# Head norm of an RWKV-7 step: mean taken off the values ahead of the scans, scale, offset and bonus in feature rows

## The chip, the cores and the metric

One core of a Trainium2 chip runs the whole step as one program. The metric is the device time of one execution in microseconds; lower is better. Three runs of the kernel before are given, and one execution was recorded by the hardware profiler.

## What is computed

One layer of a diffusion backbone on 128 context tokens and 1024 latent tokens, 1024 model columns, in float32. After a norm, one projection feeds two groups of heads: eight RWKV-7 heads of 64 (two directions), and a bidirectional RG-LRU. Their outputs are concatenated, projected, added to the input, and a gated ConvFFN follows. The change concerns the RWKV-7 heads after their scan:

```python
def _wkv7_step(S, inp):                     # S: values (i) x keys (j)
    r_t, w_t, kk_t, b_t, k_t, v_t = inp
    sa = jnp.einsum('dbhij,dbhj->dbhi', S, kk_t)
    S = S * w_t[..., None, :] - sa[..., :, None] * b_t[..., None, :] + v_t[..., :, None] * k_t[..., None, :]
    y = jnp.einsum('dbhij,dbhj->dbhi', S, r_t)
    return S, y
...
    s_fin, y = lax.scan(_wkv7_step, s0.astype(f32), xs)
    o = merge_dirs(y)
    mu = jnp.mean(o, axis=-1, keepdims=True)
    var = jnp.mean(jnp.square(o - mu), axis=-1, keepdims=True)
    o = ((o - mu) * lax.rsqrt(var + LNX_EPS)).reshape(bsz, T, WA) * lnx_g + lnx_b
    bonus = jnp.sum(rh[None] * kdh * r_k, axis=(0, -1))[..., None] * vh
    out = (o + bonus.reshape(bsz, T, WA)) * g
```

The step is linear in the values and in the first state, along the value index `i`. The latents start from a cached state; the context starts from zero, and its final states are an output.

## The kernel before

Tokens stand in nine tiles of 128 (tile 0 the context), heads in four pairs `f` of 128 features. Intermediate results go through DRAM tensors (`r_d`, `k_d`, `kk_d`, `v_d`, `kb_d`, `tt_d`, `g_d`, `y_d` and others). Most DMAs are issued by SP's queue in order, some by ACT's. Python generators mark pauses, and `beside_all` or the `Background` streams take turns among them; this sets the order in which the work is written out. The tile framework then places instructions on the engines' queues and adds all waits, so that an engine runs its own queue in order.

**Projection with background work** (`p_xwxa`, `p_k`, `p_r`, `p_v`, `p_g`). A block of the projection is 128 columns for all tokens, in three spans of 384 tokens (`SPAN`), each of 24 products. The order of the blocks' weights is in `ORDER`; `wtile` loads two blocks ahead and splits one ahead. Before, the blocks are xwxa, k0, r0, k1, r1, v0, k2, r2, v1, k3, r3, v2, v3 and the gelu blocks g0 to g2 (`EARLY`). `p_v` (L774) copies a span of values to `vt` and, with each chunk of 64 tokens reversed, to `vr`, transposes both in 128-token pieces to token rows (L788) and stores them in `v_d`. After `p_k(f)` the stream `unit_keys(f)` is pushed, after `p_r(f)` the stream `stage_ab(f)` (L521). `stage_ab` works on three groups of tokens (128, 512, 512) and two directions: rates, keys, decay powers, scaled keys, and products for the triangular inverses. `bonus` (L613) sums the keys of both directions times the queries over each head: a product with a two-column operand `rkc`, then `cols2` (L437), which copies the two rows by ACT and transposes them back to columns in `bon_f[f]`. At its end `stage_ab` pushes `inverse`, whose elimination runs on DVE. Each yield of the projection advances `stage_ab` by 4 steps, the inverses by 3, the unit keys by 2. Tiles named `ag` share 10 buffers; a group and its two directions take 9.

**Second half of the projection** (`rest_of_projection`, L965) runs beside lanes a and b of the scans: RG-LRU blocks, their gates and scans, g3, and the gate of the RWKV heads.

**Four lanes.** Each lane is a `chain` (L1074) over chunk pairs; both directions and both heads of a pair run together. First states of the latents are transposed by a product with `ident` (L1117). Beside the lanes run the rest of the modulation (`mod_rest`), the RG-LRU half of the output projection (`wout_lru`), and the posts. A post (L1251) handles two latent tiles of a head pair that both directions have completed (16 posts), or two head pairs of the context (2 posts). With tokens on the partitions it takes the mean off (L1278 to L1280), squares on ACT, sums (L1284), computes `rstd`, multiplies value by bonus (L1282) and adds the offset (L1286), multiplies by `rstd` (L1288) and scale (L1289), adds both (L1291), transposes on PE (L1295) and multiplies by the gate (L1296). It has five steps; `posts(90)` takes them in turn with the lanes, `bg_p.finish()` the rest. `PO` and `V` are both DVE.

**Output projection, second norm, FFN** follow, tile by tile in the order `seq_t`.

Of the kernel before, what the change touches and what calls it, by code (L numbers as in the profile page):

```python
# [19 lines left out]
T = 1152  # L20
# [10 lines left out]
def beside_all(*gens):  # L31
    """Advance the streams so that each has done the same share of its work."""
    st = [[g, float(n), 0] for g, n in gens]
    while st:
        s = min(st, key=lambda e: e[2] / e[1])
        try:
            next(s[0])
            s[2] += 1
            yield
        except StopIteration:  # L40
            st.remove(s)
# [17 lines left out]
def tile_hybrid_step(  # L59
# [12 lines left out]
    spill_a = nc.scalar.dma_start  # of what the activation engine has written  # L72
# [7 lines left out]
    def deal(**m):  # L80
        """Which of the eight banks each stream takes in turn."""
# [12 lines left out]
    def mm3(out, l, r, start=True, stop=True):  # L94
        """float32 product of operands given as two 12-bit parts (hi, lo)."""
# [7 lines left out]
    def round_hi(eng, hi, src):  # L103
        """src rounded to 12 bits."""
# [5 lines left out]
    def rest_lo(eng, lo, src, hi):  # L110
        """What the rounding left, which again fits into 12 bits."""
        eng.tensor_tensor(lo, src, hi.bitcast(F32), op=OP.subtract)  # L112

    def vhalf(n, d):
        """Half of the partitions that holds the values of chunk n of a pair; the other half holds the corrections."""
        return n if d == 0 else 1 - n
# [7 lines left out]
    def rstd(pool, ss, n, inv, eps, name):  # L124
        """(ss * inv + eps) ** -0.5 on [128, n], one Newton step on top of sqrt and reciprocal."""
# [21 lines left out]
    # values by chunk pair of either direction  # L147
# [5 lines left out]
    # what the first half of a chain leaves to the second: partial outputs and states  # L153
    o_d = dp.tile([4, 4, 128, 256], F32, name="o_d")
    s_d = dp.tile([4, 128, 256], F32, name="s_d")
    # per head pair and chunk pair: scaled keys and queries, and the inverses
# [14 lines left out]
    # ================================================================== first norm and input projection  # L171
# [17 lines left out]
    # of the inverses, which end later  # L189
# [31 lines left out]
    ROWS2 = [("lru_conv_w", 16), ("lru_conv_b", 4), ("ffn_conv_b", 44)]  # L221
# [38 lines left out]
    # keep: zero at the first token of each chunk, for running sums that start anew there  # L260
# [4 lines left out]
    # ------------------------------------------------------------------ conditioning columns  # L265
# [31 lines left out]
    def scaled(name, src, n, mul, add=0.0):  # L297
# [10 lines left out]
    rkc = const("rkc", 128, 4, 2)  # L308
    rkh = scaled("rkh", col("rw_r_k", 0, 4), 4, 0.5)
    V.tensor_tensor(rkc, rkh.unsqueeze(2).to_broadcast([128, 4, 2]),  # L310
                    hsel.unsqueeze(1).to_broadcast([128, 4, 2]), op=OP.mult)
    # softplus(-lam) = max(-lam, 0) + log1p(exp(-|lam|)), log1p(e) = 2 atanh(e / (2 + e))
# [21 lines left out]
    def mod_cols(idx, row, nr, n):  # L334
        """n * 128 columns of the modulation (two rows, or four with the low parts) to the partitions."""
# [16 lines left out]
    # ------------------------------------------------------------------ first norm  # L352
# [57 lines left out]
    def low_rank(f):  # L410
        """Both low-rank products' weights of a head pair: hi on both halves, lo on one."""
# [19 lines left out]
    # ------------------------------------------------------------------ RWKV: what the chains need of one head pair  # L431
    pc_f = [pc_pool.tile([128, 2, 18], F32, name=f"pc{f}") for f in range(4)]
    bon_f = [pc_pool.tile([128, 18], F32, name=f"bon{f}") for f in range(4)]
# [3 lines left out]
    def cols2(dst, src, lhs, b):  # L437
        """lhs' src, two rows, to pairs of columns."""
# [12 lines left out]
    def inverse(ds, off_, nu, done):  # L451
        """Inverses of the unit triangles of nu units per partition group, in two steps: the 32 x 32 diagonal blocks by
        elimination with one unit per partition, then the off-diagonal block."""
# [67 lines left out]
    def stage_ab(f):  # L521
        # decay, the scaled keys and queries of the chunks, and the products for the inverses
        low = low_rank(f)
        ds, off_ = ab4("ds"), iv("off", "off", 2)

        class Group:
            """Tokens of one direction: the context, or half of the latents."""
# [1305 lines left out]
```

## Time and profile before

| | us |
|---|---|
| runs of the kernel before | 1878.15, 1882.23, 1889.5 (median 1882.23) |
| span of the profiled execution | 1891.5 |
| PE busy in it | 1737.6 |
| DVE busy in it | 1327.0 |
| ACT, POOL busy in it | 850.8, 842.2 |

The span runs from the first to the last instruction of the profiled execution; the page gives no other time for that execution. PE is TensorE's products, PEld its weight loads, DVE VectorE, ACT ScalarE, POOL GpSimd, SP the queue that issues most DMAs. A product of float32 operands stands as two PE records, a transpose or a product of float32r operands as one. `mm<-h_hi,winh` names the written tile and the read ones.

### The profile page before, as it was taken

The page shows a single profiled execution, that of the slowest core. Times are in us where ns is not written, and L with a number is a line of the kernel's source. Part 1 is how long each engine was busy: PE and PEld are TensorE (multiplying, and loading weights), DVE is VectorE, ACT ScalarE, POOL GpSimd, SP SyncE. Part 2 cuts the span into 40 slices and gives each one's busy share as a digit, 9 for nine tenths or more (in the row PEclk, how much of TensorE's full clock was granted, in tenths as well). Part 3 has the DMA queues.
Part 4 walks back from the last instruction along what each step waited for, and adds up shares of the span by engine and source line. Part 5 has one row for each costly group of instructions (what it writes and reads, how often), then busy time and mean ns, then how long its engine had stood idle before and what let it go on. Part 6 is the DMA issues. An engine that isn't in the chain of part 4 may idle for free.

```text
span 1891.5 us, 36156 instructions
## 1 busy us (share of the span) xinstructions
PE 1737.6 (92%) x13421; PEld 1465.4 (77%) x13421; DVE 1327.0 (70%) x2669; ACT 850.8 (45%) x1759; POOL 842.2 (45%) x866
## 2 busy tenths in 40 slices
PE   6998899989999999789997869999999999999996
PEld 5876677778677778456664769999999999788885
DVE  5457887796567664578997967666677778567764
ACT  6345444432557467555542854444444443121211
POOL 1144554532354354353332066666666665344340
PEclk9999898888989899899996989999999999999998
DMA  8344544432533333877765412222222224648571
GB/s 251 104 151 141 161 131 155 153 125 96 164 94 116 115 101 100 261 213 241 239 190 182 152 34 85 80 77 76 71 76 71 70 82 153 191 150 272 169 253 60
DMA packets 276702, 264.94 MB, mean 140 GB/s; under 512 B 21253, under 2 KB 226720, under 8 KB 276528
## 3 DMA queue, kind: packets, MB, share of 16 engines
q1 hardware_dynamic: 260864, 245.99, 41.8%
q10 hardware_dynamic: 15376, 16.52, 2.6%
q8 instruction: 106, 1.74, 0.4%
q14 instruction: 68, 0.56, 0.1%
q0 software_dynamic: 288, 0.14, 0.0%
HBM read 188.00 MB, written 74.58 MB: 139 GB/s over the span
## 4 chain that ended last, share of the span: by engine, by line
PE 42%; DVE 4%; DMA 1%; ACT 1%; POOL 1%; issue 1%; SPq 0%; ACTq 0%; DVEq 0%; POOLq 0%
PE acc L92 13%; PE y L92 7%; PE z L92 7%; PE x L92 7%; PE v L92 3%; PE mm L92 3%; POOL wl L112 1%; PE wo L92 1%; DVE zf L1592 0%; DVE zf L1593 0%; DMA raw<-in_w_up 0%; DVE tm L1381 0%; PE tr L1455 0%; DMA act_d<-zf 0%; ACT xt L1459 0%
## 5 line engine op out<-in xcount | busy, mean ns | idle before, releaser
L92 PE MATMUL mm<-h_hi,winh 128*128 128x384 f32 x528 | 194.1, 368 | 3.4 <-DVE vr L782 2.6
L92 PE MATMUL mm<-h_lo,winh 128*128 128x384 f32 x528 | 191.2, 362 | 0.6 <-DVE h_lo L112 0.6
L92 PE MATMUL mm<-h_hi,winl 128*128 128x384 f32 x528 | 189.1, 358 | 0.0
L112 POOL TENSOR_TENSOR wl<-raw,wh 128x512 fp32r<-128x512 f32 x110 | 154.4, 1405 | 63.4 <-ACT wh L106 57.9
L106 ACT ACTIVATE wh<-raw 128x512 fp32r<-128x512 f32 x110 | 69.3, 632 | 150.3 <-PE z L92 81.0
L92 PEld LDWEIGHTS mm<-h_hi,winh 128*128 128x128 f32 x528 | 105.6, 200 | 15.8 <-issue 8.6
L92 PE MATMUL x<-f_hi,wh 128*128 128x256 f32 (+1 forms) x352 | 105.8, 301 | 9.3 <-ACT q L1625 5.6
L92 PEld LDWEIGHTS mm<-h_lo,winh 128*128 128x128 f32 x528 | 106.2, 201 | 8.5 <-issue 6.2
L112 POOL TENSOR_TENSOR wl<-S,wh 128x512 fp32r<-128x512 f32 x44 | 59.9, 1361 | 113.9 <-ACT wh L106 113.9
L92 PEld LDWEIGHTS mm<-h_hi,winl 128*128 128x128 f32 x528 | 105.8, 200 | 3.5 <-issue 2.4
L92 PE MATMUL x<-f_lo,wh 128*128 128x256 f32 (+1 forms) x352 | 105.5, 300 | 0.2 <-DVE f_lo L112 0.2
L92 PE MATMUL x<-f_hi,wl 128*128 128x256 f32 (+1 forms) x352 | 105.2, 299 | 0.0
L92 PE MATMUL y<-t_hi,wh 128*128 128x320 f32 (+1 forms) x352 | 104.5, 297 | 0.0
L92 PE MATMUL y<-t_lo,wh 128*128 128x320 f32 (+1 forms) x352 | 104.5, 297 | 0.0
L92 PE MATMUL y<-t_hi,wl 128*128 128x320 f32 (+1 forms) x352 | 104.2, 296 | 0.0
L1064 POOL TENSOR_TENSOR BK<-BK,pc 128x256 f32<-128x256 f32 x72 | 50.7, 706 | 110.8 <-PE pa L92 35.0
L108 POOL TENSOR_SCALAR winh<-win 128x512 fp32r<-128x512 f32 x44 | 29.8, 693 | 150.2 <-PE mm L92 92.4
L92 PE MATMUL acc<-f_hi 128*128 128x512 f32 x330 | 88.8, 390 | 3.3 <-ACT zf L1733 3.3
L108 POOL TENSOR_SCALAR t_hi<-raw 128x512 fp32r<-128x512 f32 x66 | 55.3, 840 | 77.1 <-PE acc L92 34.3
L1592 DVE SCALAR_TENSOR_TENSOR zf<-C,fcw,zf 128x567 f32<-128x567 f32 x66 | 63.1, 956 | 23.1 <-ACT zf L1590 23.1
L92 PEld LDWEIGHTS x<-f_hi,wh 128*128 128x128 f32 x352 | 67.8, 193 | 10.3 <-ACT q L1625 6.2
L92 PEld LDWEIGHTS acc<-f_hi 128*128 128x128 f32 x330 | 61.8, 188 | 16.4 <-ACT zf L1733 3.7
(522 smaller groups left out, 5529.0 us busy)
## 6 DMA issues: line engine op xcount, KB each, us to landing
raw<-in_w_down SPq DMA_DIRECT2D x132, 256.0 KB
raw<-in_w_up SPq DMA_DIRECT2D x88, 256.0 KB
wm<-in_w_mod SPq DMA_DIRECT2D x64, 256.0 KB
act_d<-zf SPq DMA_DIRECT2D x44, 288.0 KB
src<-act_d SPq DMA_DIRECT2D x66, 192.0 KB
win<-in_w_in SPq DMA_DIRECT2D x44, 256.0 KB
KR<-kb_d SPq DMA_DIRECT2D x36, 256.0 KB
VS<-v_d SPq DMA_DIRECT2D x36, 256.0 KB
```

The source lines that it names most:

```text
L92: PE.matmul(out, lhsT, rhs, start=start, stop=stop, skip_group_check=True)
L106: A.activation(hi, src, AF.Copy)
L108: eng.tensor_scalar(hi, src, 1.0, 0.0, op0=OP.mult, op1=OP.add)
L112: eng.tensor_tensor(lo, src, hi.bitcast(F32), op=OP.subtract)
L1064: G.tensor_tensor(bk, bk, pc_f[q.f][:, :, x:x + 1].to_broadcast([128, 2, 128]), op=OP.mult)
L1592: V.scalar_tensor_tensor(dv[:, :, 1:64], sv[:, :, 0:63], fcw[:, 0, m:m + 1], dv[:, :, 1:64], op0=OP.mult, op1=OP.add)
```

## The change

The mean over a head is taken off ahead of the scan: a matrix `cent` (identity minus 1/64 within each head) takes the place of `ident` in the transposes of the latents' values and in the product that brings in their first states; the context's values keep the identity, and its posts still take the mean off. The bonus is no longer kept as two columns per tile: a product with `rkb` (128 columns) gives it already spread over the features of its head; it is multiplied by the values in feature rows, which `p_v` now also stores (`vt_d`), and stored (`bv_d`). So `p_v(f)` comes ahead of `p_r(f)`. Scale, offset, bonus and gate of the posts are applied behind the transposes, in feature rows, where scale and offset are one number per partition: two instructions for each tile. The scale and offset columns come with the packed parameter rows. The gelu block g3 joins the early ones. Removed comments are not shown.

```diff
-    ROWS2 = [("lru_conv_w", 16), ("lru_conv_b", 4), ("ffn_conv_b", 44)]
+    ROWS2 = [("lru_conv_w", 16), ("lru_conv_b", 4), ("ffn_conv_b", 44), ("rw_lnx_g", 4), ("rw_lnx_b", 4)]
...
+    cent = const("cent", 128, 128)
+    V.tensor_copy(cent, ident)
+    for e in range(2):
+        V.tensor_scalar(cent[half(e), half(e)], cent[half(e), half(e)], 1.0 / 64.0, None, op0=OP.subtract)
...
     def stage_ab(f):
         low = low_rank(f)
         ds, off_ = ab4("ds"), iv("off", "off", 2)
+        rkb = abp.tile([128, 128], F32, name="rkb", tag="rkb", bufs=1)
+        for e in range(2):
+            V.tensor_copy(rkb[:, half(e)], hsel[:, e:e + 1].to_broadcast([128, 64]))
+        V.tensor_scalar(rkb, rkb, rkh[:, f:f + 1], None, op0=OP.mult)
...
         def bonus(g0, g1, t0):
             G.tensor_tensor(g0.kd, g0.kd, g1.kd, op=OP.add)
             G.tensor_tensor(g0.kd, g0.kd, g0.r, op=OP.mult)
-            yield
-            yield from cols2(bon_f[f][:, 2 * t0:2 * t0 + g0.W // 64], g0.kd, rkc[:, f, :], "ab")
+            bv = ag("bv")[:, 0:g0.W]
+            load(bv, vt_d[f][:, t0:t0 + g0.W])
+            yield
+            ps = bank("ab")
+            mm(ps[:, 0:g0.W], rkb, g0.kd)
+            V.tensor_tensor(bv, ps[:, 0:g0.W], bv, op=OP.mult)
+            spill(bv_d[f][:, t0:t0 + g0.W], bv)
+            yield
...
-    EARLY = range(3)
+    EARLY = range(4)
-    ORDER = [12, 4, 0, 5, 1, 8, 6, 2, 9, 7, 3, 10, 11, *[18 + q for q in EARLY]]
+    ORDER = [12, 4, 8, 0, 5, 9, 1, 6, 10, 2, 7, 11, 3, *[18 + q for q in EARLY]]
...
+            spill_a(vt_d[f][:, a:b], vt)
             yield
             for d, src in enumerate((vt, vr)):
                 ps = bank("pv")
                 for i in range(3):
-                    PE.transpose(ps[:, 128 * i:128 * i + 128], src[:, 128 * i:128 * i + 128], ident)
+                    c = slice(128 * i, 128 * i + 128)
+                    if a + i == 0:
+                        PE.transpose(ps[:, c], src[:, c], ident)
+                    else:
+                        mm(ps[:, c], src[:, c], cent)
...
-    drive(beside([p_xwxa(), p_k(0), p_r(0)], RA, RL, RI, RK))
-    drive(beside([p_k(1), p_r(1), p_v(0), p_k(2), p_r(2), p_v(1), p_k(3), p_r(3), p_v(2), p_v(3)] + [p_g(q) for q in EARLY], RA, RL, RI, RK))
+    drive(beside([p_xwxa()] + [p(f) for f in range(4) for p in (p_k, p_v, p_r)] + [p_g(q) for q in EARLY], RA, RL, RI, RK))
...
-                            mm(ps[half(e), 64 * d:64 * d + 64], s_in[half(e), d, :], ident[half(e), half(e)])
+                            mm(ps[half(e), 64 * d:64 * d + 64], s_in[half(e), d, :], cent[half(e), half(e)])
...
-    lnx = pq.tile([128, D], F32, name="lnx").rearrange("p (q c) -> p q c", q=2)
-    for i, nm in enumerate(("rw_lnx_g", "rw_lnx_b")):
-        load(lnx[:, i, :], ins[nm][0:1, :].to_broadcast([128, 512]))
...
-        V.tensor_reduce(mu[:, 0], heads(ov), axis=AX, op=OP.add)
-        V.tensor_scalar(mu[:, 0], mu[:, 0], 1.0 / 64.0, None, op0=OP.mult)
-        V.tensor_tensor(heads(ov), heads(ov), spread(mu[:, 0]), op=OP.subtract)
+        if f is None:
+            V.tensor_reduce(mu[:, 0], heads(ov), axis=AX, op=OP.add)
+            V.tensor_scalar(mu[:, 0], mu[:, 0], 1.0 / 64.0, None, op0=OP.mult)
+            V.tensor_tensor(heads(ov), heads(ov), spread(mu[:, 0]), op=OP.subtract)
         A.activation(sq, ov, AF.Square)
-        PO.tensor_tensor(heads(vt), heads(vt), spread(bon), op=OP.mult)
         yield
         V.tensor_reduce(mu[:, 1], heads(sq), axis=AX, op=OP.add)
         rv = rstd(pq, mu[:, 1].rearrange("p t e -> p (t e)"), 4, 1.0 / 64.0, 64e-5, "rv")
-        PO.tensor_tensor(vt, vt, lb, op=OP.add)
         yield
         V.tensor_tensor(heads(ov), heads(ov), spread(rv.rearrange("p (t e) -> p t e", e=2)), op=OP.mult)
-        PO.tensor_tensor(ov, ov, lg, op=OP.mult)
-        yield
-        V.tensor_tensor(sq, ov, vt, op=OP.add)
         yield
         ps = bank("po")[:, 0:256].rearrange("p (t c) -> p t c", c=128)
         for t in range(2):
-            PE.transpose(ps[:, t, :], sq[:, t, :], ident)
-        V.tensor_tensor(gt, ps, gt, op=OP.mult)
+            PE.transpose(ps[:, t, :], ov[:, t, :], ident)
+        for t, h in parts:
+            V.scalar_tensor_tensor(bv[:, t], ps[:, t], colb("rw_lnx_g", h), bv[:, t], op0=OP.mult, op1=OP.add)
+            V.scalar_tensor_tensor(gt[:, t], bv[:, t], colb("rw_lnx_b", h), gt[:, t], op0=OP.add, op1=OP.mult)
...
-    run_all((lane_a, 98 - LA), (lane_b, 98 - LB), (lane_c, 26), (lane_d, 26), (posts(90), 90),
+    run_all((lane_a, 98 - LA), (lane_b, 98 - LB), (lane_c, 26), (lane_d, 26), (posts(72), 72),
```

Here `parts` pairs each of a post's two tiles with its head pair, and `bv` is loaded from `bv_d` in place of the values.

## Rows read from the trace of the kernel before

**Rows 1.** The page's busy times: us, share of the span, instructions
```profile
PE 1737.6 (92%) x13421; PEld 1465.4 (77%) x13421; DVE 1327.0 (70%) x2669; ACT 850.8 (45%) x1759; POOL 842.2 (45%) x866
```

**Rows 2.** Windows by stage: length, busy us (records) per engine, clock, DMA share, GB/s
```profile
103.00:334.00 231.00, 205.03 (x2179) 155.73 (x2178) 175.81 (x343) 110.54 (x272) 114.28 (x147) 0.90 0.47 150
334.00:404.00 70.00, 59.78 (x697) 46.51 (x695) 58.08 (x104) 33.35 (x83) 35.45 (x50) 0.85 0.49 155
404.00:470.00 66.00, 60.19 (x716) 57.38 (x716) 51.70 (x122) 16.32 (x32) 14.19 (x21) 0.90 0.29 93
470.00:752.00 282.00, 266.06 (x2314) 213.95 (x2314) 176.72 (x358) 173.10 (x350) 128.95 (x138) 0.95 0.38 115
752.00:1022.00 270.00, 233.30 (x1781) 155.57 (x1781) 215.20 (x547) 130.87 (x320) 103.39 (x113) 0.93 0.72 224
```

**Rows 3.** Windows, the four lanes' body and their end, order PE PEld DVE ACT POOL
```profile
797.00:993.00 196.00, 182.20 (x1512) 123.05 (x1513) 167.28 (x415) 101.76 (x257) 78.28 (x84) 1.00 0.72 223
993.00:1032.00 39.00, 26.98 (x85) 17.47 (x80) 29.21 (x76) 6.85 (x16) 10.27 (x10) 0.61 0.61 195
```

**Rows 4.** Groups by line, 797 to 993: busy us, mean ns | idle before, releaser
```profile
L1282 DVE TENSOR_TENSOR v<-v,bon 128x256 f32<-128x256 f32 x15 | 10.5, 702 | 2.0 <-DMA v<-v_d 1.9
L1291 DVE TENSOR_TENSOR osq<-o,v 128x256 f32<-128x256 f32 x13 | 8.2, 634 | 0.1
L1286 DVE TENSOR_TENSOR v<-v,lnx 128x256 f32<-128x256 f32 x15 | 6.9, 463 | 0.2
L1289 DVE TENSOR_TENSOR o<-o,lnx 128x256 f32<-128x256 f32 x13 | 5.7, 439 | 0.2
L1280 DVE TENSOR_TENSOR o<-o,mu 128x256 f32<-128x256 f32 x12 | 5.4, 448 | 0.0
L1296 DVE TENSOR_TENSOR gd<-po,gd 128x256 f32<-128x256 f32 x12 | 5.0, 417 | 0.1
L1278 DVE TENSOR_REDUCE mu<-o 128x4 f32<-128x256 f32 x12 | 4.8, 406 | 0.1
L1279 DVE TENSOR_SCALAR mu<-mu 128x4 f32<-128x4 f32 x12 | 3.2, 286 | 0.0
```

**Rows 5.** Chain of waits, 752 to 1020: start us, us, what
```profile
959.05 1.59 PE wo L92 x6
...
1000.85 0.61 DVE o L1280
```

**Rows 6.** Groups by line, 797 to 993: an operation of 128 columns from PSUM
```profile
L1170 DVE TENSOR_TENSOR o<-yc,o 64x128 f32<-64x128 f32 x14 | 4.0, 288 | 0.9 <-ACT kxd L1039 0.7
```

**Rows 7.** Timeline of PE: start us, us, line, operation; 16 float32 products, three transposes
```profile
39.91 3.45 PE L92 MATMUL md<-wmod,silT 128*2 128x128 f32 x30
...
404.07 0.55 PE L788 MATMUL pv<-ident,vt 128*128 128x128 f32 x3
```

**Rows 8.** Timeline of PE, bonus transposes; waits of 103 to 470: us, times, longest
```profile
405.48 0.41 PE L447 MATMUL ab<-ident,row 2*128 2x2 f32 x4
...
DVE bon L448 <- PE ab L447: 10.6, 5, 4.1
```

**Rows 9.** Groups by line and form, DVE, 470 to 1010: 512 columns from PSUM
```profile
L1061 DVE TENSOR_TENSOR G<-pa,mask 128x512 f32<-128x512 f32 x32 | 22.0, 688 | 11.3 <-PE pa L92 10.8
```

**Rows 10.** Timeline of ACT: last span of r0; ends of two successive gelu spans
```profile
103.24 0.49 ACT L768 ACTIVATE r<-mm 128x384 f32<-128x384 f32 x1 [2.44 <-PE mm L92]
...
437.38 0.49 ACT L899 ACTIVATE gelu<-mm 128x384 f32<-128x384 f32 x1 [3.67 <-PE mm L92]
441.54 0.49 ACT L899 ACTIVATE gelu<-mm 128x384 f32<-128x384 f32 x1 [3.67 <-PE mm L92]
```

**Rows 11.** The inverses' tile: stores, ns min/median/max, first and last start us
```profile
L652 ACTq DMA_DIRECT2D tt_d<-TT x8: 326/326/338, 231.8 to 469.7; - x8
```

**Rows 12.** Waits of SP's queue, 100 to 470: us, times, longest
```profile
SPq L588 <- DVE kr L582: 53.5, 12, 10.6
```

**Rows 13.** Waits of SP's queue, 0 to 25
```profile
SPq L211 <- PE nm L375: 2.7, 1, 2.7
```

More of the change, by code (lines that the diff above doesn't have):

```diff
@@ L146, in tile_hybrid_step @@
     y_d = dp.tile([8, 128, T], F32, name="y_d")
+    vt_d = dp.tile([4, 128, T], F32, name="vt_d")
+    bv_d = dp.tile([4, 128, T], F32, name="bv_d")
     v_d = dp.tile([NT, 128, 4, 2, 128], F32, name="v_d")
@@ L307, in tile_hybrid_step @@
     gxb = scaled("gxb", col("lru_gx_b", 0, 8), 8, 0.5)
-    rkc = const("rkc", 128, 4, 2)
     rkh = scaled("rkh", col("rw_r_k", 0, 4), 4, 0.5)
-    V.tensor_tensor(rkc, rkh.unsqueeze(2).to_broadcast([128, 4, 2]),
-                    hsel.unsqueeze(1).to_broadcast([128, 4, 2]), op=OP.mult)
     lam = col("lru_lam", 0, 8)
@@ L432, in tile_hybrid_step @@
     pc_f = [pc_pool.tile([128, 2, 18], F32, name=f"pc{f}") for f in range(4)]
-    bon_f = [pc_pool.tile([128, 18], F32, name=f"bon{f}") for f in range(4)]
     dsX = abi.tile([128, 512], F32, name="dsX")
@@ L644, in stage_ab @@
                 prev = g
-            late = bonus(*gs, a // 128)
+            late = bonus(*gs, a)
         yield from prev.products()
@@ L1251, in post @@
     def post(f, p, ov):
-        vt, gt, sq = p1("v"), p1("gd"), p1("osq")
+        bv, gt, sq = p1("v"), p1("gd"), p1("osq")
         if f is not None:
             tt = slice(9 - p, p + 1, 2 * p - 9)
-            hs_ = slice(128 * f, 128 * f + 128)
-            lg, lb = [lnx[:, i, hs_].unsqueeze(1).to_broadcast([128, 2, 128]) for i in range(2)]
-            load(vt, v_d[tt, :, f, 0, :].rearrange("t p c -> p t c"))
+            load(bv, bv_d[f].rearrange("p (t c) -> p t c", c=128)[:, tt, :])
             load(gt, g_d[f].rearrange("p (t c) -> p t c", c=128)[:, tt, :])
-            bon = bon_f[f].rearrange("p (t e) -> p t e", e=2)[:, tt, :]
+            parts = [(slice(0, 2), f)]
         else:
             ov = ov.rearrange("p (t c) -> p t c", c=128)[:, 2 * p:2 * p + 2, :]
-            lg, lb = [lnx[:, i, 256 * p:256 * p + 256].rearrange("p (f c) -> p f c", f=2) for i in range(2)]
-            load(vt, v_d[0, :, 2 * p:2 * p + 2, 0, :])
+            load(bv, bv_d[2 * p:2 * p + 2, :, 0:128].rearrange("f p t -> p f t"))
             load(gt, g_d[2 * p:2 * p + 2, :, 0:128].rearrange("f p t -> p f t"))
-            bon = pq.tile([128, 2, 2], F32, name="bonX", tag="bonX", bufs=2)
-            for i in range(2):
-                V.tensor_copy(bon[:, i, :], bon_f[2 * p + i][:, 0:2])
+            parts = [(slice(i, i + 1), 2 * p + i) for i in range(2)]
         def heads(ap):
```

## Prediction

> **What bounds the kernel now.** I read the page's busy times first [rows 1]: PE 92% of the span, DVE 70%, the others under half. The chain of waits is PE alone from 1105 us on, in the two FFN stages, which the change does not touch. So I cut the time before into stages [rows 2]: projection with background work (103 to 470 us), second half of the projection beside lanes a and b (470 to 752), four lanes with posts, modulation and output weights (752 to 1022). In the first, PE is busy 89% (205.0 of 231, 59.8 of 70, 60.2 of 66), DVE 76 to 83%, at a mean granted clock of 0.85 to 0.90: neither alone is the limit, both nearly are. From 470 PE is busy 94%. In the last stage PE and DVE share the limit; cut finer [rows 3], 797 to 993 shows PE 93% and DVE 85% at full clock, but 993 to 1032 shows DVE 29.2 of 39, PE 27.0 at a clock of 0.61. The chain of waits in order of time says the same: PE pieces up to 990, then almost only DVE pieces, among them post steps that the change removes [rows 5].
>
> **Posts (removal).** A latent post loses eight DVE instructions: sum (L1278), scaling (L1279), subtraction (L1280), bonus product (L1282), offset (L1286), scale (L1289), sum (L1291), gate product (L1296). By the means of [rows 4] that is 0.406 + 0.286 + 0.448 + 0.702 + 0.463 + 0.439 + 0.634 + 0.417 = 3.80 us. It gains four scalar_tensor_tensor of 128 columns, two of them reading PSUM. The trace before has none; the nearest row is a DVE operation of 128 columns from PSUM, 0.288 us [rows 6], so 1.15 us; by twice that row (a third operand, contention with POOL) 2.3. Net 2.65 us (1.5 to 2.65), times 16 latent posts = 42 us (24 to 42). The two context posts keep the mean and run first, while the lanes fill, so I count nothing for them.
>
> What this is worth depends on the place. *Body, 797 to 993:* [rows 4] has 12 posts there, 32 us of DVE. PE's work in the stage is unchanged (same transposes of the posts), and PE has 196 − 182.2 = 13.8 us of idle in all. Part of that is caused by POOL, ACT and DMA, so I take 5 us, bounds 0 and 14. *Tail, 993 to 1032:* the last four posts stand in DVE's queue among the output weights' splits, and PE waits. 3 to 4 posts × 2.65 us = 8 to 10 us; one instruction of each post now waits for PE's transposes later in the chain, so I take 7, bounds 3 and 14 (14 if PE, less starved, also keeps its clock at 2.4 GHz; at 0.61 it ran mostly at 1.2). Sum −12 us, bounds −3 and −28. The posts' steps fall from 90 to 72, four for each post instead of five, spread over the stage as before: nothing.
>
> **Centring the values (addition).** 64 of the 72 transposes in `p_v` become float32 products with `cent`. A transpose is one PE record of 128 columns: three of them take 0.55 us, and a run of records ends in a modelled tail of some 0.2, so about 0.11 each [rows 7]. A float32 product of 128 columns is two records of 0.115 each (30 in 3.45 us, [rows 7]). So 0.115 us more for each, 64 × 0.115 = 7.4 us on PE, 0 if it hides and 14.7 at half clock. With PE 89% busy I count 6.6. The Trainium skill, Trace Analysis, Transposes, says that logical transposes should use transpose mode and not a standard matmul; by that rule the swap costs, as the record pairs show too; read alone, it would make the whole change some 7 us slower, which leaves out what the swap takes from DVE later. Eight transposes of context tiles and the initial states' products (already with a matrix operand) cost the same as before. `cent` itself is three small DVE operations in the first microseconds, nothing.
>
> **Bonus in feature rows.** Removed for each of 12 groups: ACT's row copy, a small DVE copy, and transposes of two rows, 36 in all (four in 0.41 us, some 0.07 each beyond the tail [rows 8], −2.5 us of PE); and with them a round trip from PE over ACT and PE to DVE, for whose end DVE sat idle 10.6 us [rows 8]. Added: a DVE product with PSUM, 0.69 us for 512 columns [rows 9], 8 × 0.69 + 4 × 0.29 = 6.7 us; 12 small operations for `rkb`, some 1.5 as an estimate; 12 issues on ACT's queue, in place of 12 row copies; 12 loads and 12 spills on SP. Net on PE −2.5, on DVE at most +8.2, waits some −3 of the 10.6. DVE is 78% busy over the stage (285.6 of 367 us, [rows 2]), so I count 2 of the 8.2 (0 to 8). SP already waits 53.5 us in all for DVE before the scaled keys' spills, because it issues in order [rows 12]; the new spill of `bv` adds a wait of the same kind in front of these spills, the next loads of `rk` and the weight loads, which run two blocks ahead; cover as before, nothing (up to 5 if it delays `rk`). The pool of 10 `ag` tiles is now full with 10 per group instead of 9; same bounds. Centring and bonus together: 6.6 − 2.5 − 3 + 2 = +3 us, bounds −6 and +18.
>
> **Order of the projection.** All values move in front of their `r`, and the last gelu block (g3) moves from the stage after 470 to the one before. `stage_ab(0)` starts when r0 ends, at 103 us before [rows 10]; now one value block stands ahead of that: a block is three spans of 4.16 us [rows 10] plus transposes, so 15 us later. Afterwards the foreground has 13 blocks either way, and the last `stage_ab` has four light gelu blocks beside it instead of two value and three gelu blocks. g3 takes 3 × 4.16 = 12.5 us out of the stage that is 94% PE. If PE sets both stages, its work is only moved, and the two cancel: I take +15 − 12.5 = +2.5 us. Bounds: −10 if the tail of `stage_ab(3)` and the inverses shortens by as much as the start is late; +18 in the rival below.
>
> **Ahead of that and after.** One more small load on SP at the start: SP then waits 2.7 us for PE before the last input tile anyhow [rows 13], which covers it (uncovered some 1 us). Two broadcast loads of `lnx` go. The second norm and the FFN keep their work.
>
> **Sum.** −12 + 3 + 2.5 = −6.5 us, about −7 with the two loads. The profiled execution has a span of 1891.5 us, 9.3 above the median of the three runs (1882.2; the page shows no time for it beyond the span), so the result is 1884.5 on that scale, and 1882.2 × 1884.5 / 1891.5 = 1875 us as a median.
>
> **Rivals.** *DVE's relief pays in full.* PE's busy time counts modelled ends, and its weight loads fill only 123 of 196 us in the body [rows 3]. Were DVE the limit there, 32 us less of it would shorten the body by 15 to 25 us, the tail by 7 or more: −27 + 5.5, some −21, so 1861 us. The Trainium skill, Trace Analysis, Identifying the Most-Contended Engine, says that matmul busy share is no good measure and to judge TensorE by its weight loads; by that rule (63% here) DVE is the limit and this rival holds. Against it: the chain has PE pieces back to back from 951 to 963 us, of lanes, output weights and modulation alike (one of them in [rows 5]), so the trace agrees only in part.
> *The late start is not paid back (slower).* The lanes start when the last inverse is stored, at 470 us [rows 11]: their tiles take the place of the inverses'. The chain r3, `stage_ab(3)`, two inverses was 136 us long, and r3 ended at 334, where I cut the stages. Now r3 has two more value blocks ahead of it. If the last store is more than 15 us later (mechanism: 15 for the first value block, up to 15 for the rest), and lanes a and b, not PE, set the stage after, g3's removal returns little: +25 − 8 + 3 − 12 = +8, up to +18: 1890 to 1900. It decides from a last store at about 490 us with the next stage longer than 272.
> *The edit is made and nothing moves*: DVE's relief is eaten by PE's extra work: 1880 to 1884.
>
> **How the numbers follow.** Forecast (1868 to 1881) 0.45, full relief (1850 to 1867) 0.23, not paid back (1886 to 1900) 0.20, nothing moves 0.12. A measurement here tells about 0.5%, 9.4 us: faster is below 1872.8, slower above 1891.6. Faster: 0.23 and two fifths of 0.45 = 0.41. Slower: three quarters of 0.20 = 0.15. The rest 0.44. Range 1853 to 1893: it leaves out the ends of both outer cases; the forecast alone is 1868 to 1881.
>
> **What would show it.** Posts: four DVE operations of about 0.29 us each, DVE busy in the 196 us before the tail down by some 30, PE idle there still about 10. Tail: less than 39 us between the lanes' end and the steady output projection. Values: two records for each product, 7 us more PE. Order: r0 ends near 118, the last inverse is stored between 470 and 485, and the next stage is 10 to 13 us shorter. I am wrong if the body shrinks by over 14 us (PE was not its limit), or if the lanes start after 490.

## The result, and the profile after

| | us |
|---|---|
| kernel before, median beside it (seven runs, the three given ones among them) | 1888.9 (1878.2 to 1891.9) |
| changed kernel, median | 1899.4 (1893.4 to 1906.4) |
| ratio of the two, 95% interval | 1.0058 (1.0036 to 1.0080) |
| span of the profiled execution, before and after | 1891.5, 1897.1 |

The changed kernel is slower by 0.6%, some 11 us; 1875 was forecast, with 1893 as the upper end. The profiled execution of before was a long one (a second one has a span of 1884.6), so the two spans differ by less than the medians. The page's busy times, where [rows 1] stood:

```profile
PE 1731.8 (91%) x13449; PEld 1469.9 (77%) x13449; DVE 1295.0 (68%) x2581; ACT 856.0 (45%) x1757; POOL 835.3 (44%) x867
```

DVE has 88 instructions and 32 us less; the forecast's terms give 34 (42 off in the posts, 8 added). PE is not busier, though some 5 us more were forecast for it (7.4 for the products, 2.5 off). So neither engine's total tells why the time rose.

The stages are cut at marks that both kernels have: the projection's first product, the last store of the inverses (`tt_d`), the second context post's store, the first product of the output projection's second half, its last product. Windows of the kernel before by these marks (length, then busy us and records of PE, PEld, DVE, ACT, POOL, then clock, DMA share, GB/s):

```profile
0.00:58.20 58.20, 41.81 (x346) 31.71 (x346) 34.60 (x115) 33.72 (x65) 9.16 (x23) 1.00 0.85 243
58.20:469.70 411.50, 368.13 (x3822) 297.82 (x3822) 301.90 (x594) 176.15 (x412) 167.66 (x222) 0.90 0.42 133
469.70:805.70 336.00, 308.20 (x2616) 242.20 (x2614) 204.00 (x439) 204.22 (x421) 147.38 (x162) 0.93 0.44 135
805.70:995.90 190.20, 174.63 (x1437) 117.31 (x1436) 164.98 (x406) 94.84 (x239) 75.49 (x81) 1.00 0.72 223
995.90:1081.60 85.70, 72.63 (x294) 53.62 (x294) 72.20 (x177) 47.47 (x112) 9.46 (x9) 0.82 0.51 170
1081.60:1891.50 809.90, 772.18 (x4915) 722.71 (x4913) 549.32 (x943) 294.42 (x512) 433.03 (x370) 0.98 0.37 116
```

The same windows of the changed kernel:

```profile
0.00:60.90 60.90, 44.00 (x347) 34.09 (x347) 36.40 (x120) 34.08 (x65) 9.58 (x24) 0.97 0.79 232
60.90:516.10 455.20, 401.84 (x4009) 332.08 (x4008) 315.19 (x617) 197.04 (x430) 172.62 (x230) 0.91 0.44 141
516.10:825.80 309.70, 272.03 (x2415) 211.33 (x2413) 185.80 (x404) 185.78 (x394) 137.78 (x151) 0.93 0.45 135
825.80:1013.00 187.20, 176.47 (x1477) 120.12 (x1477) 141.19 (x338) 98.75 (x248) 76.18 (x84) 1.00 0.74 229
1013.00:1087.50 74.50, 65.18 (x293) 49.69 (x294) 66.83 (x162) 46.58 (x111) 8.15 (x9) 0.93 0.62 201
1087.50:1897.10 809.60, 772.23 (x4915) 722.61 (x4913) 549.64 (x943) 293.75 (x512) 430.96 (x370) 0.98 0.37 116
```

I call the six stages start, projection, lanes a and b, four lanes, output, FFN. Start is 2.7 us longer, projection 43.7 longer, lanes a and b 26.3 shorter, four lanes 3.0 shorter, output 11.2 shorter, FFN unchanged. The first three together lost 20.1, the next two gave 14.2 back. Subtract PE's busy time from the length and the loss has a place: PE's idle time rose from 43.4 to 53.4 us in the projection and from 27.8 to 37.7 us beside lanes a and b.

The rest of the projection's extra length is mostly work that moved: 4009 records against 3822 stand ahead of the last store, and 2415 against 2616 behind it. While the lanes waited for the inverses, PE ran products of the RG-LRU blocks ahead.

The rows that answer to [rows 10] and [rows 11], the last span of r0 (ACT's timeline) and the stores of the inverses:

```profile
124.03 0.49 ACT L782 ACTIVATE r<-mm 128x384 f32<-128x384 f32 x1 [3.67 <-PE mm L92]
```

```profile
L666 ACTq DMA_DIRECT2D tt_d<-TT x8: 326/326/327, 223.5 to 516.1; - x8
```

r0 ended 20.8 us later, the last store came 46.4 us later. The answers to [rows 3], the 196 us before the lanes' end and the 39 us behind it, and to [rows 4], the groups of DVE by form in the first of them (busy us, mean ns | idle before):

```profile
814.00:1010.00 196.00, 186.55 (x1549) 125.90 (x1549) 145.33 (x347) 105.94 (x266) 80.32 (x89) 1.00 0.73 226
1010.70:1049.70 39.00, 30.07 (x125) 21.86 (x124) 32.84 (x81) 16.81 (x40) 9.51 (x10) 0.87 0.78 240
```

```profile
L1303 DVE SCALAR_TENSOR_TENSOR gd<-v,colB,gd 128x256 f32<-128x256 f32 x11 | 8.0, 723 | 0.2
L1302 DVE SCALAR_TENSOR_TENSOR v<-po,colB,v 128x256 f32<-128x256 f32 x11 | 5.3, 481 | 2.6 <-PE po L1300 2.5
```

DVE is busy 145.3 of 196 us instead of 167.3, PE 186.6 instead of 182.2. The 39 us of what was the tail now have a clock of 0.87 instead of 0.61.

Waits of the changed kernel, 61 to 516 us (us, times, longest), where [rows 8] had DVE waiting 10.6 us for the bonus's transposes:

```profile
PE ab L92 <- DVE bv L629: 10.0, 5, 3.3
DVE bv L629 <- PE ab L92: 1.1, 1, 1.1
```

DVE's wait is nearly gone, and PE has one of the same size, ahead of the next product that needs the bank (`ab`): the bank that holds the product stays taken until the multiplication has its turn in DVE's queue.

### The profile page after: what moved, and what is told of

The parts are those of the page before. It is cut to its first block, busy times and chain, and to the rows that moved or that the text cites. A ratio compares the mean times of both kernels' runs of the same rounds, so it can differ in the third digit from the quotient of the medians.

```text
span 1897.1 us, 36229 instructions
## 1 busy us (share of the span) xinstructions
PE 1731.8 (91%) x13449; PEld 1469.9 (77%) x13449; DVE 1295.0 (68%) x2581; ACT 856.0 (45%) x1757; POOL 835.3 (44%) x867
## 3 DMA queue, kind: packets, MB, share of 16 engines
q1 hardware_dynamic: 263528, 250.19, 42.5%
## 4 chain that ended last, share of the span: by engine, by line
PE 65%; DVE 13%; issue 7%; POOL 6%; DMA 4%; ACT 4%; SPq 0%; DVEq 0%; ACTq 0%; POOLq 0%
PE acc L92 13%; PE mm L92 8%; PE x L92 7%; PE z L92 7%; PE y L92 7%; PE v L92 4%; PE md L92 2%; PE ya L92 2%; DVE gt L466 2%; DVE X L468 2%; PE pa L92 2%; PE lg L92 2%; PE wo L92 2%; PE yb L92 1%; PE ca L92 1%
## 5 line engine op out<-in xcount | busy, mean ns | idle before, releaser
L1599 DVE SCALAR_TENSOR_TENSOR zf<-C,fcw,zf 128x567 f32<-128x567 f32 x66 | 63.4, 960 | 24.2 <-ACT zf L1597 24.1
L112 DVE TENSOR_TENSOR t_hi<-raw,t_hi 128x512 fp32r<-128x512 f32 x66 | 48.2, 736 | 39.1 <-POOL t_hi L108 39.1
```

The source lines that it names most:

```text
L1599: V.scalar_tensor_tensor(dv[:, :, 1:64], sv[:, :, 0:63], fcw[:, 0, m:m + 1], dv[:, :, 1:64], op0=OP.mult, op1=OP.add)
```

## The experiments

All times stand beside the kernel before, run on the same chip; "ratio" is to it. "Projection" is the stage from its first product to the last `tt_d` store. Two profiled executions of the kernel before agree to 0.7 us in the end of every block up to r3 and to 0.2 us in this stage (411.5, 411.7), but differ by 4.3 us beside lanes a and b and by 2.5 in the output stage. Not every pair agrees so well: e3 and e15 are the same program up to the last store, but for one place in ACT's queue, and their projections took 404.9 and 407.5 us, at clocks of 0.93 and 0.91. So a difference of less than some 3 us in a stage shows nothing. I read the causes from the projection stage, and the worth of a kernel from its ratio; where the next stage takes back what the projection gave, I say so.

**e1_old_order.** The whole change in the old order of blocks:

```diff
-    ORDER = [12, 4, 8, 0, 5, 9, 1, 6, 10, 2, 7, 11, 3, *[18 + q for q in EARLY]]
+    ORDER = [12, 4, 0, 5, 1, 8, 6, 2, 9, 7, 3, 10, 11, *[18 + q for q in EARLY]]
...
-            V.tensor_tensor(bv, ps[:, 0:g0.W], bv, op=OP.mult)
-            spill(bv_d[f][:, t0:t0 + g0.W], bv)
+            A.activation(bv, ps[:, 0:g0.W], AF.Copy)
+            spill_a(bs_d[f][:, t0:t0 + g0.W], bv)
```

> All of the change but its order: blocks, EARLY and drive as in the kernel before. The bonus is stored ahead of the multiplication by the values, and a stream of its own behind p_v(f) loads both, multiplies (12 operations of 384 columns on DVE) and stores bv. Late-start theory (the new order puts the last inverse 46 us later, and that is not paid back): last tt_d store back at 470 to 480 us, the lanes' end before 990, time 1870 to 1882 us, 15 to 30 below the changed kernel. New-work theory (products with cent, the bonus and the posts cost what was lost): time within 6 us of the changed kernel, 1893 to 1905.

Measured: 1895.9 us, ratio 1.0037 (1.0015 to 1.0059); last store 490.3. The time is the one that the new-work theory expected; the last store misses the late-start theory's 470 to 480, but is far from the changed kernel's 516: the old order gives back 26 of the 46 us, yet the time falls by only 3 or 4. The projection is 430.1 us where the old work in this order takes 411.5. So the order is not the whole loss, and the new work ahead of the lanes costs something too. How much, e1 may overstate, since its stream behind `p_v` brings loads and stores of its own.

**e2_new_order.** The kernel before with `ORDER`, `EARLY` and `drive` of the changed one, and nothing else.

> The kernel before with only the order of the changed one (ORDER, EARLY, drive); posts, bonus and transposes as before. Late-start theory: last tt_d store at 505 to 515 us, and time 1898 to 1912 us, slower than the changed kernel or equal to it, since the posts' relief is missing. New-work theory: 1884 to 1893, no change.

Measured: 1900.1 us, ratio 1.0060 (1.0039 to 1.0081). Its projection and its stage beside lanes a and b:

```profile
58.00:503.80 445.80, 403.32 (x3993) 325.08 (x3993) 310.74 (x609) 201.80 (x442) 168.17 (x230) 0.91 0.40 128
503.80:815.70 311.90, 273.13 (x2412) 210.54 (x2411) 185.55 (x414) 185.21 (x395) 141.24 (x153) 0.93 0.45 137
```

The last store is 34 us late, and the next stage is only 24 shorter. PE's idle time in the projection is 42.5 us, as before the change (43.4); beside lanes a and b it is 38.8 instead of 27.8. The order alone costs 11 us, and this is where. In time the late-start theory holds for it; the expectation of 505 to 515 for the last store was missed by 1 us.

**e3_g3_early.** The kernel before with `EARLY = range(4)`.

> The kernel before with only g3 among the early gelu blocks. If g3's 12.5 us of PE only move from one stage to the other: 1885 to 1893. If they fill PE while the last inverses hold the lanes back, and leave a stage that PE limits: last tt_d store 0 to 5 us later, 1874 to 1884. If the inverses get later by all of it: 1893 to 1900.

Measured: 1883.7 us, ratio 0.9970 (0.9952 to 0.9989). Of the kernels that leave nothing out it is the only one that is faster than both. The time is that of the second expectation, the reason given there is not: the last store came 6.8 us earlier, not later. Its stage beside lanes a and b, PE's largest wait in it (us, times, longest), and the projection's products alone in this stage (tile `mm`: PE, PEld, DVE, ACT, then clock, DMA share, GB/s), of the kernel before and of e3:

```profile
462.90:798.90 336.00, 302.58 (x2583) 237.66 (x2582) 202.97 (x437) 195.60 (x414) 147.55 (x164) 0.93 0.44 134
```

```profile
PE lg L92 <- POOL sgh L108: 8.2, 1, 8.2
```

```profile
469.70:805.70 336.00, 79.33 (x395) 69.05 (x393) 20.47 (x42) 10.32 (x17) 0.93 0.44 135
462.90:798.90 336.00, 80.29 (x395) 67.14 (x393) 22.50 (x48) 10.45 (x17) 0.93 0.44 134
```

The stage is as long as before, 336.0 us, and it holds as many of the projection's products, 395. So g3's 72 did not leave it. Before, PE had run 38 products of the next block ahead while the lanes waited for the last store (1190 stood ahead of it, of which the 16 early blocks are 1152); in e3 g3 stands in that place and itself ends at 470.0 us, 7 us behind the store. PE now waits 8.2 us for POOL's rounding of the RWKV gate's rows (`sgh`), ahead of the gate's products. Before, g3's products stood there and covered it: PE has this wait in every kernel here with g3 early, the changed one too, and in none with g3 late (before, its second execution, e1). What it costs is not shown, since e3 is the faster kernel. The gain lies in the projection (404.9) and the output stage (79.1); its cause stays open, but in the projection the same 3822 records take PE 359.1 us instead of 368.1, at a clock of 0.93 instead of 0.90.

**e4_transposes.** The changed kernel with `PE.transpose(ps[:, c], src[:, c], ident)` for all values, so that the latents' mean stays in.

> The changed kernel with plain transposes of the values in place of the products with cent, so that the mean over a head is never taken off the latents. Late-start theory: the four value blocks get 1.8 us shorter each, last tt_d store 506 to 512, time 1892 to 1897. New-work theory: the products are the larger part of the loss, 1885 to 1891.

Measured: 1904.1 us, ratio 1.0072 (1.0047 to 1.0097), projection 453.6. Both expectations are missed: taking the products away shortens the projection by 1.6 us, which shows nothing, and the time not at all. PE is busy 3.3 us less in that stage, and by groups the products and transposes of the values take 14.1 us of PE in place of 22.8, so the products cost PE something that nothing waits for. The latents' mean stays in, so this kernel is for the time alone.

**e5_bonus_pool.** The changed kernel with the multiplication on POOL:

```diff
-            V.tensor_tensor(bv, ps[:, 0:g0.W], bv, op=OP.mult)
+            A.activation(g0.kd, ps[:, 0:g0.W], AF.Copy)
+            G.tensor_tensor(bv, g0.kd, bv, op=OP.mult)
```

> The changed kernel, but ACT copies the bonus out of PSUM and POOL multiplies it by the values, so that the PSUM bank no longer waits for its turn in DVE's queue. Bank theory (in the changed kernel PE waited 10.0 us for the bonus multiplication on DVE): those waits fall under 3 us, last tt_d store at 505 to 511 us, time 1889 to 1895. Rival (the bonus costs by its loads, stores and the tenth tile): 1897 to 1903.

The reason was PE's wait of 10.0 us above. Measured: 1909.2 us, ratio 1.0123 (1.0095 to 1.0151), projection 465.6. PE's wait for `bv` is gone, and the stage is 10 us longer, PE idle 55.1 as against 53.4. The bank theory falls: the wait was only where the delay showed. POOL took the 1.27 us per multiplication (median) into the chain of each group, and itself waits 9.3 us there for ACT's copies.

**e6_no_bonus.** The changed kernel without `rkb`, the product and `bv_d`; the posts add the plain values.

> The changed kernel without the bonus product: no operand rkb, no multiplication, no bv loads and stores beside the projection; the posts add the plain values, so the bonus factor is left out. POOL's two operations stay. If the bonus edit is what the changed kernel loses against the old work in the new order (stage to the last tt_d store 455 against 446 us): last store 503 to 508, time 1886 to 1893. If the products with cent or the start are: 1896 to 1901.

Measured: 1889.8 us, ratio 1.0024 (1.0006 to 1.0042), projection 449.0, so 6.2 us shorter. Taken alone this would look like the price of the edit; by e14 the old form of the bonus has a price of this size too.

**e7_lnx_apart.** The changed kernel with the rows of scale and offset out of `ROWS2`, loaded and transposed ahead of the posts.

> The changed kernel with the scale and offset rows loaded and transposed by themselves just ahead of the posts, not in the packed rows of the start. Start theory (two more small loads ahead of the modulation weights): first product of the projection at 58.0 to 58.5 us as without them, 2 to 3 us earlier than in the changed kernel, time 1895.5 to 1897.5. Rival (the later start is a matter of single executions): first product at 60 to 62, time 1898 to 1901.

Measured: 1898.6 us, ratio 1.0064 (1.0044 to 1.0085). The projection's first product starts at 58.52 us, in the changed kernel at 60.85. The mark is back, as the start theory says. The time is not: its projection took 458.0. Over all kernels here, the first product comes at 59.4 to 61.5 us where these rows are in the packed load (six kernels) and at 57.8 to 59.5 where they are not, about 2 us apart.

**e8_parts.** Old order, g3 early, rows apart, products with `cent`, new posts; ACT copies the bonus out of PSUM, POOL multiplies it in the post.

> The parts put together the other way: posts and mean of the changed kernel, g3 early, but block order and drive of the kernel before, scale and offset rows loaded apart, the bonus copied out of PSUM by ACT and stored without the values, and multiplied by them on POOL inside the post. If order, start and the bonus's place are what ate the posts' relief: 1872 to 1882 us, faster than the kernel before; last tt_d store 463 to 475. If the new posts give no relief of their own: 1883 to 1890.

Measured: 1889.4 us, ratio 1.0005 (0.9987 to 1.0022), projection 416.1, output 78.5. The time is that of the second case, no relief: it is no faster than before, though order and start are gone. Its output stage is no shorter than e3's (79.1), and against e3 the projection is 11.2 us longer.

**e9_best.** As e8, with a tile of its own for the bonus and the multiplication on POOL beside lanes a and b:

```diff
-        yield from beside([gens[e[0]](*[int(c) for c in e[1:]]) for e in SEQ], 0, RL, 0)
+        bg_a.push(bonus_values())
+        yield from beside([gens[e[0]](*[int(c) for c in e[1:]]) for e in SEQ], 0.5, RL, 0)
```

> As e8_parts, but the bonus has a tile of its own and is multiplied by the values on POOL beside lanes a and b, where the old order leaves slack, so the posts are those of the changed kernel. If e8_parts lost its posts' relief to the tenth tile of the ring and to the multiplication in the posts: stage to the last tt_d store 403 to 410 us, the output projection 74 to 76, time 1872 to 1880 us. If neither matters: 1885 to 1891.

Measured: 1890.3 us, ratio 1.0018 (1.0004 to 1.0032); projection 417.5, lanes a and b 341.3, output 74.0. The output stage is as short as in the changed kernel, so POOL's multiplication in the posts had cost e8 some 1 to 4 us there (e17, also without it, has 77.2). The projection did not move, and lanes a and b, which now have the multiplication beside them, took 6 us longer than in e8 (335.3; two executions of the kernel before differ by 4.3 there).

**e10_tile_parts, e11_tile_after.** e8 and the changed kernel, each with only this:

```diff
-            bv = ag("bv")[:, 0:g0.W]
+            bv = abp.tile([128, 512], F32, name="bv", tag="bv", bufs=2)[:, 0:g0.W]
```

> As e8_parts, with the one difference that the bonus has a tile of its own and no longer a tenth place in the ring that the next group's loads wait for. Ring theory: stage from the projection's first product to the last tt_d store 403 to 410 us instead of 416, time 4 to 10 us below e8_parts. Rival (the bonus costs by its product and its copy or the values' stores): 413 to 419, time within 3 us of e8_parts.

> The changed kernel with the one difference that bv has a tile of its own. Ring theory: stage to the last tt_d store 446 to 450 us instead of 455, as with the old bonus in the new order, time 1890 to 1895. Rival (it is the multiplication's place in DVE's queue): 453 to 458, 1897 to 1902.

Measured: e10 1897.4 us, ratio 1.0057 (1.0040 to 1.0074), projection 419.8; e11 1903.9, ratio 1.0108 (1.0089 to 1.0127), projection 455.0. The ring theory falls, and both got slower than their bases (by 0.5%), which the rivals did not expect either. Though one tile is all that was edited, PE's records of e8 and e10 stand in another order at many places from some 371 us on. I have no mechanism for the 0.5%.

**b2_before_again.** The kernel before, once more.

> The kernel before once more, for how far two profiled executions of one program lie apart stage by stage: start 58, projection to the last tt_d store 405 to 412, lanes a and b 336, four lanes 190, output projection and second norm 79 to 86, FFN 809 to 811. If the first profile was a typical one, each stage is within 2 us of it.

Measured: 1886.8 us; start 57.8, projection 411.7, lanes a and b 331.7, four lanes 190.3, output 83.2, FFN 809.9. Lanes a and b and the output stage repeat less well than that.

**e12 to e14.** Three parts alone, each on e3: e12 adds only `spill_a(vt_d[f][:, a:b], vt)` in `p_v`; e13 has the bonus through `rkb`, copied by ACT and stored, in place of `cols2`; e14 has no bonus product at all.

> The kernel before with g3 early, and only the stores of the values in feature rows added (one store for each span on ACT's queue). Stage from the projection's first product to the last tt_d store was 404.9 us with g3 early and 416 to 420 with the values' stores, products with cent and bonus in feature rows together. If the stores hold ACT's queue or the tiles: 409 to 414. If they cost nothing: 404 to 407, time as with g3 early, 1881 to 1886.

> The kernel before with g3 early and the bonus in feature rows as in e8_parts (rkb, one product, a copy by ACT, a store), transposes and values as before; the posts use the factor one, so the bonus is left out of the output. If this form of the bonus is the cost in the projection: 411 to 416 us to the last tt_d store. If the products with cent or the values' stores are: 404 to 407.

> The kernel before with g3 early and no bonus product at all, old or new; POOL's two operations stay, the posts use the factor one, so the bonus is left out. If either form of the bonus lies on the path: 395 to 400 us to the last tt_d store, by its product of some 0.6 us for each record and its round trip. If the old form is hidden: 403 to 406.

Their projections (windows), e12, e13, e14:

```profile
58.20:469.70 411.50, 367.82 (x3821) 295.40 (x3820) 296.68 (x586) 176.57 (x412) 167.84 (x219) 0.90 0.43 139
```

```profile
58.00:463.40 405.40, 357.76 (x3786) 291.12 (x3786) 298.06 (x583) 176.09 (x412) 170.66 (x219) 0.91 0.44 141
```

```profile
58.00:454.90 396.90, 344.82 (x3748) 286.31 (x3747) 299.75 (x574) 170.71 (x399) 166.97 (x219) 0.91 0.43 137
```

The stage without these edits took 404.9 us in e3 and 407.5 in e15, which is the same program up to there. So with the stores it is 4 to 6.6 us longer, with the bonus by product, copy and store no longer (405.4), and without any bonus 8 to 11 shorter (396.9). e13 copies the bonus by ACT, so it does not hold the changed kernel's multiplication on DVE. That the stores hold something up is not shown by e12: PE's idle time in the stage is 43.7 us, against 45.8 in e3 and 42.2 in e15, and what grew is the busy time of the same records, at a clock of 0.90. And the shorter projection of e14 is not kept: its next stage took 343.7 us, and the two stages together 740.6, against 740.9 in e3 and 746.0 in e15. Its time is lower than e3's by 0.3%, with intervals that overlap. Times of e12, e13, e14: 1888.5 (ratio 0.9996, 0.9970 to 1.0022), 1883.1 (0.9983, 0.9957 to 1.0008), 1876.0 (0.9941, 0.9916 to 0.9965).

**e15_posts_only.** e3 with scale, offset and gate behind the transposes, but mean and bonus as before, values times bonus transposed beside the rows:

```diff
-        PO.tensor_tensor(heads(vt), heads(vt), spread(bon), op=OP.mult)
+        G.tensor_tensor(heads(vt), heads(vt), spread(bon), op=OP.mult)
...
+            PE.transpose(pv[:, t, :], vt[:, t, :], ident)
+        A.activation(sq, pv, AF.Copy)
```

> The kernel before with g3 early and posts of a mixed kind: mean and bonus as before, with the bonus multiplication on POOL, values times bonus transposed beside the rows, scale, offset and gate behind the transposes. Nothing changes ahead of the lanes. If the posts' relief is what the change has to give: four lanes 186 to 188 us, output projection and second norm 74 to 77, time 1875 to 1881, faster than the kernel before. If POOL's multiplication in the post eats it: 1882 to 1887.

Measured: 1887.0 us, ratio 0.9995 (0.9972 to 1.0018); four lanes 190.4, output 79.8. DVE is 12.6 us less busy in the four lanes than in e3 (153.7 against 166.4), and the stage is no shorter. So DVE did not set it, unless what the edit adds to the posts (two transposes, a copy, POOL's multiplication) took back as much.

**e16_store_sp, e17_best_sp.** e12 and e9 with `spill` in place of `spill_a` for the values.

> As e12_vt_store, with the stores of the values issued on SP's queue in place of ACT's. If the twelve stores cost by their place on ACT's queue (0.33 us each between the copies that PE waits for): stage to the last tt_d store back from 411.4 to 405 to 408 us. If they cost by what they hold (the tile, the DMA engines): 410 to 413. If SP, which issues in order, waits for the copies and holds up the loads behind: over 413.

> As e9_best, with the stores of the values on SP's queue. If ACT's queue was the price: stage to the last tt_d store 410 to 414 us instead of 417.5, time 1883 to 1888. If not: 416 to 420 and 1888 to 1893.

Measured: e16 1891.3 us, ratio 1.0029 (1.0008 to 1.0050), projection 410.0; e17 1890.9, ratio 1.0022 (1.0003 to 1.0041), projection 415.9. ACT's queue was not the price: on SP's the stage is as long. PE's idle time in e16's projection is 47.1 us, so here something may wait; what, stays open. In time, e16 is 0.6% behind e3 with intervals apart, e12 0.3% with intervals that overlap.

## Why the prediction was wrong, step by step

**Order: this step failed.** "If PE sets both stages, its work is only moved, and the two cancel: I take +15 − 12.5 = +2.5 us." Measured: +11 us for the order alone (e2). Two parts of it broke.
- *The return.* The 12.5 us of g3 were to leave a stage in which PE was 94% busy. They did not leave it: with g3 early (e3) as many projection products stand behind the last store as before, 395, since PE had been running that stage's products ahead while the lanes waited, and g3 took their place. Where work did leave the stage, the stage did not shorten by as much: in e2 PE is busy 35.1 us less there (273.1 against 308.2), and it is 24.1 us shorter. So being 94% busy did not mean that PE sets its length; 8.2 us of PE's new idle time is the wait for `sgh`, a round trip that g3 had covered and for which the prediction gave no cover.
- *The start.* +15 is the delay of r0, and was right for it; but the last store hangs on r3, which has two more value blocks ahead of it, and is what counts. With the order alone (e2) r0 ends 16.0 us later, r3 22.1, and the last store comes 34.1 later. In the changed kernel r0 ended 20.8 us later: 2.7 from the start, 19.4 for the value block (12.5 of spans, and the transposes and unit keys beside them), less 1.3. From there to r3 came another 20, and 5 more to the last store: 46 in all. In both kernels the gelu blocks, the last of the early ones, end some 40 us ahead of the last store (462.0 and 503.8 in e2), where it was 19 before (450.4 and 469.7): fewer blocks are left beside the last `stage_ab` and its inverses. That this is what makes the end late was not run by itself. PE used the time for RG-LRU products, so those were not lost; but beside lanes a and b PE idled 10 to 11 us more. This is near the rival "the late start is not paid back". Half of its mark is passed (last store 516 against 490), the other half is not (the next stage was to shorten by less than 10 us, and by the marks used here shortened by 26); it forecast 1890 to 1900, and had a chance of 0.20.

e3 says that g3 alone is worth −6 us; the values ahead of `r` then cost some 17, a difference of two runs and not run by itself.

**Centring and bonus: in bounds, wrong terms.** Counted +3 (−6 to +18). In the new order, projection and lanes a and b took 764.9 us instead of 757.7 (after against e2): +7. By parts: the bonus in its new form costs 6.2 us of stage (e6), in its old form 8 to 11 (e14), and product, copy and store alone no more than the old form (e13): −4 to 0, and −3.5 was counted. The products cost 0 to 5: e4 shows 1.6 us of stage and nothing in the time, e8 shows 4.6 beyond the stage with the stores; 6.6 were counted. The term that was left out is the stores of the values: "12 issues on ACT's queue, in place of 12 row copies" was priced at nothing, and the stage with them is 4 to 6.6 us longer (e12), on either queue; how much of that is the clock stays open. The Trainium skill, Perfetto Trace Analysis, Transposes, asks for the transpose mode; here the rule shows in the records (4009 against 3966 in the projection), not in the time.

**Start: failed, small.** "Which covers it": not covered. First product 2 us later with the two rows in the packed load. PE waited 2.9 us for modulation weights (0.9 before). In the time the 2 us did not show (e7).

**Posts: mechanism right, the body too large.** Forecast −5 in the body, −7 in the tail. I had read four operations of 128 columns for a post; there are two of 256 columns for latent posts (two for both tiles together, not for each), 0.48 + 0.72 = 1.20 us against the 1.15 counted, so the saving was right. A nearer row than the one taken stood in the trace before: the scalar_tensor_tensor `xc<-mm`, 0.34 us for 127 columns from PSUM. DVE's busy time in the 196 us fell by 22, not 30. The four lanes' stage got 3.0 shorter here; over eight profiles with the old posts it is 189.1 us in the mean (186.1 to 191.8), over nine with the new ones and no multiplication by POOL in the post 188.3 (186.2 to 191.5). So −3 by this pair and −1 by the means, which is less than either group's spread. The output stage over the same profiles is 81.1 in the mean with the old posts (77.9 to 85.7) and 74.8 with the new (73.9 to 77.2): −6, as forecast; part of it is the clock, 0.93 instead of 0.82. The rival "relief in full" (weight loads, not busy share, decide; DVE the limit) is out: it wanted 15 to 25 us, and 12.6 (e15) and 24 us less of DVE (the change) shortened the four lanes by 0 and 3.

**A reading that was off.** The chain of waits is not PE alone from 1105 us on: it has DMA, POOL and DVE pieces up to 1137. Nothing rests on it.

**The sum.** Order +11, stores +5, products 0 to 5, bonus −4 to 0, start 0 to +2, posts −7 to −9: +3 to +16. The terms behind the order are stage lengths of single executions, so this is an account and no proof. Measured +11 (+7 to +15). Forecast −7. Of the 24 us between 1875 and 1899, 4 to 7 are the median of before, which was 1882.2 in three runs and 1885.9 to 1888.9 beside the kernels here.

**What stays open.** Why the order alone makes the last store 34 us late when r3 is 22 late; why e3 gains; whether the values' stores hold anything up in the projection, or the clock makes it longer; why giving `bv` its own tile made two kernels 0.5% slower; how the old order with all parts (e8, e9, e17) loses 8 to 13 us of projection, of which the stage with the stores has about half. The wait that was removed in e5 came back under another name.

## What to carry to other kernels

Before counting on work to leave a stage, count what stands in it before and after: where the engine already runs the next stage's work ahead, an early block may only change the order. Name also what the block covers where it stands, and do not take a busy share for a limit: beside lanes a and b, with PE over 90% busy, 35 us less of its work gave 24 us. Work put ahead of the start of a long dependent chain has to be priced at the chain's end, not at its start: here the first block was 16 us late, the last one 22 and the last store 34. New stores for data that was never stored before deserve a term of their own, and a removed wait, or one shorter stage, proves nothing until the time gets shorter.

## What was not expected of the hardware

Up to r3, at 334 us, block ends repeat to 0.7 us between the two executions of the kernel before, while its output stage differs by 2.5 us with the clock (0.82 and 0.86). That is not the rule: e3 and e15, with the same records in the same order on PE, end r3 at 331.4 and 335.3 us.

The scalar_tensor_tensor of 256 columns whose first operand is in PSUM took 467 to 488 ns in all 16 posts of latents. The one that reads only SBUF took 457 to 486 ns in eleven of them and 0.68 to 1.59 us in the other five. In each of those five a GpSimd operation on weights (`wml`, `woh` or `wl`) ran beside it, for 0.9 to 1.3 us of the four longest; of the eleven only one had such a neighbour for more than 0.02 us, and took 457 ns. So the means in the rows above, 723 and 481 ns, are not two prices: the medians of all 20 operations of each line are 485 and 478.
